# Rotary embedding on one core: the first slab loaded by one transfer instead of four

## The chip, the core and the metric

The kernel runs on one core of a Trainium2 chip. The metric is the device time of one execution in microseconds (us); three executions of the kernel before gave 164.84, 165.05 and 165.22 us, median 165.05. One of them, the 164.84 us one, was also recorded by the hardware profiler, and every line of the profile here is from it.

## The reference

`x` has 16 batches, 512 positions and 1024 values, which are 16 heads of 64; `cos` and `sin` are 512 x 32. All are float32, and so is the output.

```python
x = x.reshape(batch, seq, num_heads, head_dim)
x1, x2 = x[..., :half_dim], x[..., half_dim:]
cos = cos[None, :, None, :]
sin = sin[None, :, None, :]
rotated = np.concatenate([x1 * cos - x2 * sin,
                          x1 * sin + x2 * cos], axis=-1)
```

Every value is read once, takes part in two products and one sum, and is written once: 33.5 MB in and 33.5 MB out.

## The kernel before

**Tiling.** Two batches (`nb` = 2) make a slab: 1024 positions, of which each of the 128 partitions holds 8 in a row. A slab's row in one partition is 8 x 1024 floats, 32 KB, and lies in one piece in memory; a slab is 4 MB. There are 8 slabs and 5 buffers for them (`slots` = 5), and a slab's result is written over its input in the same buffer. A slab is worked in two passes of 4 positions, 16 passes in all.

**A pass** (L130 to L147). ScalarE casts half a slab from float32 to bf16 (L124, "xb"). VectorE multiplies it by the sin table into `t2` and by the cos table in place (L137, twice), and adds the two with the halves of `t2` exchanged (L140). ScalarE casts the result back to float32 into the slab (L144). After a slab's second pass ScalarE issues the slab's store (L146), one 4 MB transfer. The cast of the next pass is issued ahead of the current one (L131), so ScalarE's order is: cast of pass i+1, cast back of pass i.

**Tables** (L80 to L115). cos and sin are loaded by GpSimd's queue (L82), cast to bf16 (L99), spread over the partitions by four small matmuls with a 0/1 matrix (L103) and copied to SBUF as [cos cos] and [sin -sin] (L109 to L115).

**Queues.** Loads of slabs 1 to 7 are issued by SyncE (SP), one transfer of 128 rows each (L65). Loads of slabs 1 to 4 are issued at the start; the load of slab s+5 is issued after the pass that ends slab s (L148), and waits until the store of slab s has landed, since it goes into the same buffer. Stores are issued by ScalarE's queue. Each queue runs in order; transfers of the two queues share 16 DMA engines.

**The first slab** (L69 to L75). Its load is cut into four transfers by rows: the 64 even rows on SP's queue, rows 7, 15, 23, ... (16 rows) on ScalarE's queue, rows 1, 5, 9, ... (32 rows) and then rows 3, 11, 19, ... (16 rows) on SP's queue. All four go into the one tile `slab[0]`, and the first cast waits for all of them.

Of the kernel before, what the change touches and what calls it, by code (L numbers as in the profile page):

```python
# [2 lines left out]

# [4 lines left out]


@with_exitstack  # L10
def kernel(
    ctx: ExitStack,
    tc: tile.TileContext,
    x: bass.AP,
    cos: bass.AP,
    sin: bass.AP,
    num_heads: int,
    out: bass.AP,
):
    nc = tc.nc  # L20
    P = nc.NUM_PARTITIONS

    batch, seq, dim = x.shape
    nh = num_heads
    hd = dim // nh
    half = hd // 2
    bf16 = mybir.dt.bfloat16
    f32 = mybir.dt.float32

    nb = 2  # L30
    slots = 5
    nslabs = batch // nb
    rpp = nb * seq // P
    W = rpp * dim
    SP = seq // rpp
    rows = 4
    PW = rows * dim
    TW = rpp * half

    out_flat = out.rearrange("b s h d -> b s (h d)")  # L40

    singles = ctx.enter_context(tc.tile_pool(name="singles", bufs=1))
    slabs = ctx.enter_context(tc.tile_pool(name="slabs", bufs=slots))
    tpool = ctx.enter_context(tc.tile_pool(name="tpool", bufs=3))
    t2pool = ctx.enter_context(tc.tile_pool(name="t2pool", bufs=2))
    psum = ctx.enter_context(tc.tile_pool(
        name="psum", bufs=1, space=bass.MemoryType.PSUM))


    def dram(t, s, a=0, n=W):  # L50
        return bass.AP(tensor=t.tensor, offset=t.offset + s * nb * seq * dim + a,
                       ap=[[W, P], [1, n]])


    def view(t, offset, *dims):
        return dataclasses.replace(t, offset=t.offset + offset,
                                   ap=[t.ap[0], *[list(d) for d in dims]])


    slab = {}  # L60


    def load(s):
        slab[s] = slabs.tile([P, W], f32, tag="slab", name="slab")
        nc.sync.dma_start(out=slab[s], in_=dram(x, s))  # L65

    slab[0] = slabs.tile([P, W], f32, tag="slab", name="slab")  # L69
    for q, first, step in ((nc.sync, 0, 2), (nc.scalar, 7, 8),  # L70
                           (nc.sync, 1, 4), (nc.sync, 3, 8)):
        q.dma_start(  # L72
            out=slab[0][first::step, :],
            in_=bass.AP(tensor=x.tensor, offset=x.offset + first * W,
                        ap=[[step * W, P // step], [1, W]]))  # L75


    TR = seq // P
    G = rpp // TR
    raw = singles.tile([P, 2 * TR * half], f32, tag="raw")  # L80
    for i, src in enumerate((cos, sin)):
        nc.gpsimd.dma_start(out=view(raw, i * TR * half, (1, TR * half)), in_=bass.AP(  # L82
            tensor=src.tensor, offset=src.offset,
            ap=[[TR * half, P], [1, TR * half]]))

    for s in range(1, slots):
        load(s)


    pick = singles.tile([P, G * P], bf16, tag="pick")  # L90
    nc.gpsimd.memset(pick, 0.0)  # L91
    for g in range(G):
        part = view(pick, g * P, (SP, P // SP), (1, SP))
        nc.gpsimd.affine_select(  # L94
            out=part, in_=part, compare_op=mybir.AluOpType.not_equal, fill=1.0,
            base=-g, pattern=[[0, P // SP], [-G, SP]], channel_multiplier=1)

    tab1 = singles.tile([P, 2 * TR * half], bf16, tag="tab1")
    nc.vector.tensor_copy(out=tab1, in_=raw)  # L99
    acc = psum.tile([P, 2 * TW], f32, tag="acc")  # L100
    for i in range(2):
        for g in range(G):
            nc.tensor.matmul(view(acc, i * TW + g * TR * half, (1, TR * half)),  # L103
                             view(pick, g * P, (1, P)),
                             view(tab1, i * TR * half, (1, TR * half)),
                             start=True, stop=True)

    tab = singles.tile([P, 2 * rpp * hd], bf16, tag="tab")
    nc.vector.tensor_copy(out=view(tab, 0, (hd, 2 * rpp), (1, half)),  # L109
                          in_=view(acc, 0, (half, 2 * rpp), (1, half)))  # L110
    nc.vector.tensor_copy(out=view(tab, half, (hd, rpp), (1, half)),  # L111
                          in_=view(acc, 0, (half, rpp), (1, half)))
    nc.vector.tensor_scalar_mul(  # L113
        out=view(tab, rpp * hd + half, (hd, rpp), (1, half)),
        in0=view(acc, TW, (half, rpp), (1, half)), scalar1=-1.0)  # L115


    xb = {}


    def cast(u):
        s, k = u
        xb[u] = tpool.tile([P, PW], bf16, tag="xb", name="xb")
        nc.scalar.copy(out=xb[u], in_=view(slab[s], k * PW, (1, PW)))  # L124

    passes = [(s, k) for s in range(nslabs) for k in range(rpp // rows)]
    cast(passes[0])
    for i, u in enumerate(passes):  # L130
        if i + 1 < len(passes):  # L131
            cast(passes[i + 1])
        s, k = u
        xs, xu = slab[s], xb.pop(u)
        t2 = t2pool.tile([P, PW], bf16, tag="t2")
        for t, a in ((t2, rpp * hd), (xu, 0)):
            nc.vector.tensor_mul(  # L137
                out=t, in0=xu,
                in1=view(tab, a + k * rows * hd, (hd, rows), (0, nh), (1, hd)))
        nc.vector.tensor_add(  # L140
            out=xu, in0=xu,
            in1=view(t2, half, (hd, rows * nh), (-half, 2), (1, half)))

        nc.scalar.copy(out=view(xs, k * PW, (1, PW)), in_=xu)  # L144
        if k == rpp // rows - 1:
            nc.scalar.dma_start(out=dram(out_flat, s), in_=xs)  # L146
            if s + slots < nslabs:  # L147
                load(s + slots)  # L148


# [1 line left out]
_INS = ['x', 'cos', 'sin', 'num_heads']  # L152
_OUTS = [((16, 512, 16, 64), 'float32')]

_NUMBERS = {'num_heads': 16}


# [26 lines left out]
```

## Time and profile before

| | |
|---|---|
| time, median of 3 | 165.05 us |
| the profiled execution | 164.84 us |
| its span, first to last instruction | 162.9 us |
| around the span | 1.94 us |
| VectorE busy | 111.3 us, 68% |
| ScalarE busy | 114.8 us, 70% |
| TensorE, GpSimd busy | 0.6 us, 2.3 us |
| DMA | 67.24 MB, mean 413 GB/s over the span |
| one cast, either way | 3.60 us, 32 of them |
| one VectorE operation of a pass | 2.29 us, 48 of them |

The page of the profile gives busy times by engine, the span in 40 slices with the DMA engines' busy share and rate, the DMA queues (q1 is SP's, q10 ScalarE's, q0 GpSimd's), the chain of work that ended last, groups of instructions, and DMA issues. Answers on a stretch of the span are of three kinds: windows (busy time of each engine, the DMA engines' busy share and rate, where a DMA packet counts wholly in the window in which it starts), a timeline, and the chain in order of time. DMA packets of this kernel are rows: one 32 KB row is one packet on one of the 16 DMA engines.

### The profile page before, as it was taken

What the parts mean: (1) busy time and instruction counts of PE and PEld (TensorE: products, weight loads), DVE (VectorE), ACT (ScalarE), POOL (GpSimd) and SP (SyncE); (2) the same over time, 40 slices, a digit from 0 to 9 for tenths busy, and PEclk for the clock granted to TensorE, in tenths of its full rate; (3) what the DMA queues carried; (4) which work ended last, traced back from release to release, by engine and by line L of the source; (5) the groups of instructions that cost most, each with busy time, mean ns of one, the idle gap of its engine ahead of it and who ended that gap; (6) DMA issues with size and microseconds to landing.
All of it is one profiled execution on the core that took longest, in us unless ns stands there. A gap on an engine that the chain in (4) does not pass through costs nothing.

```text
span 162.9 us, 188 instructions
## 1 busy us (share of the span) xinstructions
PE 0.6 (0%) x4; PEld 0.4 (0%) x4; DVE 111.3 (68%) x52; ACT 114.8 (70%) x33; POOL 2.3 (1%) x9
## 2 busy tenths in 40 slices
PE   0000000000000000000000000000000000000000
PEld 0000000000000000000000000000000000000000
DVE  0003069999899999999999999907996099940000
ACT  0000997779999999999999999169980899553000
POOL 5000000000000000000000000000000000000000
DMA  5999899898998998998989989989989899899893
GB/s 169 354 410 258 386 491 410 386 515 386 402 499 386 451 451 386 483 418 386 515 386 402 499 386 443 459 386 491 410 386 515 386 410 491 386 459 443 386 491 153
DMA packets 2416, 67.24 MB, mean 413 GB/s; under 512 B 336, under 2 KB 336, under 8 KB 368
## 3 DMA queue, kind: packets, MB, share of 16 engines
q10 hardware_dynamic: 1184, 34.08, 49.0%
q1 hardware_dynamic: 1168, 33.03, 48.5%
q0 software_dynamic: 64, 0.13, 0.3%
HBM read 33.69 MB, written 33.55 MB: 413 GB/s over the span
## 4 chain that ended last, share of the span: by engine, by line
DMA 45%; ACT 25%; DVE 13%; issue 6%; SPq 1%; ACTq 0%
DMA slab<-in_x_dram 25%; DMA out_dram<-slab 21%; ACT slab L144 15%; ACT xb L124 9%; DVE t L137 4%; DVE xb L140 4%; DVE xb L137 4%; ACT L124 1%; SPq L72 1%; ACTq L144 0%; ACTq L124 0%; SPq L65 0%
## 5 line engine op out<-in xcount | busy, mean ns | idle before, releaser
L124 ACT CAST xb<-slab 128x4096 bf16<-128x4096 f32 x16 | 57.5, 3601 | 11.0 <-DMA slab<-in_x_dram 11.0
L144 ACT CAST slab<-xb 128x4096 f32<-128x4096 bf16 x16 | 57.7, 3603 | 5.5 <-DVE xb L140 5.3
L137 DVE TENSOR_TENSOR t<-xb,tab 128x4096 bf16<-128x4096 bf16 x16 | 36.7, 2292 | 19.6 <-ACT xb L124 19.2
L140 DVE TENSOR_TENSOR xb<-xb,t 128x4096 bf16<-128x4096 bf16 x16 | 36.7, 2292 | 0.5
L137 DVE TENSOR_TENSOR xb<-xb,tab 128x4096 bf16<-128x4096 bf16 x16 | 36.7, 2292 | 0.5
L124 ACT ACT_TABLE_LOAD x1 | 1.3, 1283 | 16.7 <-DMA slab<-in_x_dram 16.7
L99 DVE CAST tab<-raw 128x256 bf16<-128x256 f32 x1 | 0.3, 294 | 11.7 <-DMA raw<-in_sin_dram 11.7
L109 DVE CAST tab<-acc 128x512 bf16<-128x512 f32 x1 | 0.7, 691 | 0.7 <-PE acc L103 0.7
L82 POOL DMA_DIRECT2D raw<-in_cos_dram x1 | 0.7, 677 | 0.8 <-POOLq L165 0.8
L103 PE MATMUL acc<-tab,pick 128*128 128x128 bf16 x4 | 0.6, 302 | 12.0 <-DVE tab L99 12.0
L94 POOL TENSOR_SCALAR_AFFINE_SELECT pick<-pick 128x128 bf16<-128x128 bf16 x2 | 0.5, 289 | 0.1
L82 POOL DMA_DIRECT2D raw<-in_sin_dram x1 | 0.5, 534 | 0.0
L103 PEld LDWEIGHTS <-pick 128*128 128x128 bf16 x4 | 0.4, 128 | 11.9 <-issue 8.7
L111 DVE CAST tab<-acc 128x256 bf16<-128x256 f32 x1 | 0.4, 415 | 0.0
L113 DVE TENSOR_SCALAR tab<-acc 128x256 bf16<-128x256 f32 x1 | 0.4, 414 | 0.0
L91 POOL MEMSET pick<- 128x256 bf16 x1 | 0.3, 330 | 0.0
L165 POOL MEMSET const-bfloat16-1.0<- 128x1 bf16 x1 | 0.1, 103 | 0.0
L165 POOL MEMSET const-float32-0.0<- 128x1 f32 x1 | 0.1, 99 | 0.2 <-issue 0.2
L165 POOL MEMSET const-uint8-127<- 128x1 uint8 x1 | 0.1, 102 | 0.0
L165 POOL MEMSET const-float32-1.0<- 128x1 f32 x1 | 0.1, 99 | 0.0
## 6 DMA issues: line engine op xcount, KB each, us to landing
out_dram<-slab ACTq DMA_DIRECT2D x8, 4096.0 KB, 28.2
slab<-in_x_dram SPq DMA_DIRECT2D x7, 4096.0 KB, 25.7
slab<-in_x_dram SPq DMA_DIRECT2D x1, 2048.0 KB, 10.7
slab<-in_x_dram SPq DMA_DIRECT2D x1, 1024.0 KB, 12.8
slab<-in_x_dram ACTq DMA_DIRECT2D x1, 512.0 KB, 9.2
slab<-in_x_dram SPq DMA_DIRECT2D x1, 512.0 KB, 14.6
raw<-in_cos_dram POOLq DMA_DIRECT2D x1, 64.0 KB, 8.9
raw<-in_sin_dram POOLq DMA_DIRECT2D x1, 64.0 KB, 9.7
```

Of the source, the lines that this page charges most:

```text
L72: q.dma_start(out=slab[0][first::step, :], in_=bass.AP(tensor=x.tensor, offset=x.offset + first * W, ap=[[step * W, P // step], [1, W]]))
L82: nc.gpsimd.dma_start(out=view(raw, i * TR * half, (1, TR * half)), in_=bass.AP(tensor=src.tensor, offset=src.offset, ap=[[TR * half, P], ...
L94: nc.gpsimd.affine_select(out=part, in_=part, compare_op=mybir.AluOpType.not_equal, fill=1.0, base=-g, pattern=[[0, P // SP], [-G, SP]], c ...
L103: nc.tensor.matmul(view(acc, i * TW + g * TR * half, (1, TR * half)), view(pick, g * P, (1, P)), view(tab1, i * TR * half, (1, TR * half)) ...
L109: nc.vector.tensor_copy(out=view(tab, 0, (hd, 2 * rpp), (1, half)), in_=view(acc, 0, (half, 2 * rpp), (1, half)))
L111: nc.vector.tensor_copy(out=view(tab, half, (hd, rpp), (1, half)), in_=view(acc, 0, (half, rpp), (1, half)))
L113: nc.vector.tensor_scalar_mul(out=view(tab, rpp * hd + half, (hd, rpp), (1, half)), in0=view(acc, TW, (half, rpp), (1, half)), scalar1=-1.0)
L124: nc.scalar.copy(out=xb[u], in_=view(slab[s], k * PW, (1, PW)))
L137: nc.vector.tensor_mul(out=t, in0=xu, in1=view(tab, a + k * rows * hd, (hd, rows), (0, nh), (1, hd)))
L140: nc.vector.tensor_add(out=xu, in0=xu, in1=view(t2, half, (hd, rows * nh), (-half, 2), (1, half)))
L144: nc.scalar.copy(out=view(xs, k * PW, (1, PW)), in_=xu)
L165: nc = _bacc.Bacc("TRN2", target_bir_lowering=False, num_devices=1)
```

## The change

The four transfers of the first slab become one of 128 rows on SP's queue, by the same function that loads the other slabs. Nothing else differs: `t2` has two buffers before and after.

```diff
-    slab[0] = slabs.tile([P, W], f32, tag="slab", name="slab")
-    for q, first, step in ((nc.sync, 0, 2), (nc.scalar, 7, 8),
-                           (nc.sync, 1, 4), (nc.sync, 3, 8)):
-        q.dma_start(
-            out=slab[0][first::step, :],
-            in_=bass.AP(tensor=x.tensor, offset=x.offset + first * W,
-                        ap=[[step * W, P // step], [1, W]]))
+    load(0)
```

`load(s)` is the function at L63: it takes a slab buffer and issues `nc.sync.dma_start(out=slab[s], in_=dram(x, s))`.

In the compiled order of instructions VectorE, TensorE and GpSimd have the same instructions in the same order as before. SP issues five whole-slab loads at the start in place of three pieces and four loads. ScalarE's queue loses its one load, and its table load (the instruction ahead of its first cast) no longer has a wait for three of the four pieces in front of it; the wait for the slab stands at the first cast.

## The prediction

> **What bounds the kernel now.** I began with the page's slices, because neither VectorE (68%) nor ScalarE (70%) is busy enough to set the time. Lines of slices and queues:
>
> ```profile
> DMA  5999899898998998998989989989989899899893
> GB/s 169 354 410 258 386 491 410 386 515 386 402 499 386 451 451 386 483 418 386 515 386 402 499 386 443 459 386 491 410 386 515 386 410 491 386 459 443 386 491 153
> ...
> q10 hardware_dynamic: 1184, 34.08, 49.0%
> q1 hardware_dynamic: 1168, 33.03, 48.5%
> q0 software_dynamic: 64, 0.13, 0.3%
> ```
>
> The reader is to see that the 16 DMA engines are busy from about 2 us to the end: 49.0 + 48.5 + 0.3 = 97.8% of the span. So only three things can move the time: when the DMA engines start, when they run dry, and how long a row takes on them. The fourth slice (12.2 to 16.3 us), 258 GB/s, is the one slow slice inside a busy stretch. I therefore cut the span into windows whose edges fall between rounds; a **round** is one 32 KB row on each of the 16 engines, 0.524 MB. The last columns are the DMA engines' busy share and GB/s:
>
> ```profile
> 2.00:5.15 3.15, 0.00 (x0) 0.10 (x1) 0.00 (x0) 0.00 (x0) 1.30 (x4) 1.00 0.97 333
> 5.15:7.00 1.85, 0.00 (x0) 0.00 (x0) 0.00 (x0) 0.00 (x0) 0.00 (x0) 1.00 1.14 283
> 7.00:12.95 5.95, 0.59 (x4) 0.32 (x3) 0.59 (x2) 0.00 (x0) 0.00 (x0) 1.00 0.96 375
> 12.95:14.95 2.00, 0.00 (x0) 0.00 (x0) 1.05 (x3) 0.00 (x0) 0.00 (x0) 1.00 1.09 262
> 14.95:16.80 1.85, 0.00 (x0) 0.00 (x0) 0.00 (x0) 0.12 (x1) 0.00 (x0) 1.00 0.92 283
> 16.80:36.20 19.40, 0.00 (x0) 0.00 (x0) 14.52 (x7) 16.44 (x6) 0.00 (x0) 1.00 1.00 432
> ...
> 148.00:161.20 13.20, 0.00 (x0) 0.00 (x0) 0.00 (x0) 0.00 (x0) 0.00 (x0) 1.00 0.93 400
> ```
>
> From 16.80 to 36.20, whole slabs alone move 432 x 19.4 = 8.38 MB, 16 rounds, so a **normal round takes 19.4 / 16 = 1.21 us**. Ahead of 16.80 there are rounds that take far longer with the engines fully busy: the engines are held up inside rows, not waiting for work. A row's time in a window of one round is its share x its length: 1.14 x 1.85 = 2.11 us in the second line. That round is ScalarE's transfer, by the queue line of the same window:
>
> ```profile
> DMA packets 16, 0.52 MB, mean 283 GB/s; under 512 B 0, under 2 KB 0, under 8 KB 0
> ...
> q10 hardware_dynamic: 16, 0.52, 114.0%
> ```
>
> Last I read the end. The chain of waits goes through load 7, its two passes and the last cast:
>
> ```profile
> 101.00 25.66 DMA slab<-in_x_dram
> ...
> 144.36 3.60 ACT slab L144
> ```
>
> The last store is issued at 148.00. From there to 161.20 the engines still move 400 x 13.2 = 5.28 MB; the last store is 4.19 MB. So 1.09 MB of the store before it, two rounds that have yet to start and one that is running, keep the engines busy until about 151.5: the end is set by the engines' total work, and the chain through load 7 has about 3.5 us, less the delay from issue to first row, in hand. That delay, by the first load (issued at 0.74, first rows in the window that begins at 2.00), is about 1.4 us: **2.1 us in hand**.
>
> **The change, part by part.**
>
> *The two 16-row pieces go.* In rounds, the first slab takes: even rows 4, ScalarE's piece 1, rows 1::4 two, rows 3::8 one, 8 in all. By order in the queue, 12.95 to 14.95 is the round of rows 3::8 and 14.95 to 16.80 the first of slab 1, which starts unevenly behind it.
> - ScalarE's round: 2.11 - 1.21 = 0.90 us lost.
> - Rows 3::8: 1.09 x 2.00 = 2.18; lost 0.97.
> - The round behind: 0.92 x 1.85 = 1.70; lost 0.49.
> - 7.00 to 12.95: q1's four rounds there take 87.4% of 5.95 = 5.20 us in place of 4.85; 0.35 lost. The tables' small packets run in it and are not removed; I give 0.10 of it to them and 0.25 to the round behind ScalarE's.
>
> Sum: 0.90 + 0.97 + 0.49 + 0.25 = **2.6 us**. Only the 16-row pieces, on two different queues, have slow rounds; the 64 rows, the 32 rows and the whole slabs do not, so I charge the shape, not the queue or the moment. The new load has the shape of slabs 1 to 4, 16 rounds of which ran at 1.21. Nothing hides this loss and nothing hides its return, as all later rounds follow without a hole.
>
> [...]
>
> *The first round stays.* The window 2.00 to 5.15 holds two rounds in 3.15 us, where 2.42 would do: up to 0.7 us of starting cost. The whole-slab load has no row at a cold start. Below, it could start like an even-rows load and cost the same; a gain of 0.6 if that start is also of the split's making; a loss of 0.6 if 128 rows take twice as long to get going. SP's issue instruction took 0.56 to 0.59 us for 64, 32 and 16 rows alike, so I take 0.
>
> *Issues.* SP issues three fewer (about 0.6 us each), so loads 1 to 4 are queued some 2 us earlier; the queue in front of them is never empty, so this is worth nothing. ScalarE loses an issue of 0.57 us, which lies in a wait of 16 us: nothing.
>
> *The compute chain moves by more than the transfers.* ScalarE's timeline:
>
> ```profile
> 16.68 1.28 ACT L124 ACT_TABLE_LOAD   x1 [16.68 <-DMA slab<-in_x_dram]
> 17.97 7.11 ACT L124 CAST xb<-slab 128x4096 bf16<-128x4096 f32 x2
> 26.21 3.60 ACT L124 CAST xb<-slab 128x4096 bf16<-128x4096 f32 x1 [1.13 <-DMA slab<-in_x_dram]
> ...
> 38.88 0.35 ACTq L146 DMA_DIRECT2D out_dram<-slab  x1
> ```
>
> Slab 0's rows end, by rounds: two by about 5.3, six more at 1.21, 0.5 for the tables' packets: 13.1; slab 1's landing stood 0.7 behind its last row, so 13.8 in place of 16.6. The 1.28 us table load leaves the path, as it no longer stands behind a wait. First cast: 13.8 instead of 17.97, 4.2 earlier; VectorE's tables, ready at 14.0 before, are wanted at 17.4. The first store is issued at about 34.7, 4.2 earlier, and thus 1.6 us (one to two rounds) earlier in the stream of transfers. From there the queues take turns, so loads 3 to 7 end one or two rounds later in the stream: load 7 lands 2.6 - 1.2 = 1.4, or 2.6 - 2.4 = 0.2 us, earlier than before. The last store's issue follows it by 21.3 us as now: 146.6 or 147.8. Its first row is due at 151.5 - 2.6 = 148.9 and can start 1.4 behind the issue, at 148.0 or 149.2. So this is hidden, or costs 0.3.
>
> Forecast: 164.84 - 2.6 = 162.2 for the profiled execution; that one stands 0.2 below the median of its three, so **162.4** for the median.
>
> **Rivals.**
> 1. *Part of it stays.* ScalarE's slow round may be the first use of its queue, and come back with the first store: 0.90 + 0.25 kept, 165.05 - 1.46 = 163.6. For: it is the queue's first transfer. Against: the other 16-row piece is as slow on a queue long in use.
> 2. *The tail shows.* Load 7 comes two or three rounds later in the stream: the last store starts 0.3 to 1.5 late, 162.7 to 163.9. For: 2.1 us in hand is little.
> 3. *The change does not do it.* The slow rounds belong to the moment (tables' packets, PSUM copies from 12.65 to 14.0) and stay: 165.0, no change. Against: VectorE is busier later with rounds at 1.21.
> 4. *Slower.* The same tail, further: the first store comes so early that load 7 is pushed back by five rounds or more in the stream: 126.65 - 2.6 + 5 x 1.21 = 130.1, the last store's issue 151.4, first row 152.8 in place of 151.5: 166.4. It decides from about 4.2 rounds. For: each round that the first store gains pushes load 7 back by one. Against: that takes a first store some 6 us earlier in the stream, and VectorE's chain lets it gain 1.6.
>
> **How the numbers follow.** Forecast 0.70, rival 1 0.10, rival 2 0.09, rival 3 0.06, rival 4 0.05. Changes under 0.2% (0.33 us) are about what a measurement of this kernel cannot tell from none. Faster 0.89, same 0.06, slower 0.05. The range takes in the forecast with the starting round's 0.6 either way, most of rival 2 and rival 1: 161.6 to 163.6.
>
> **What would show it.** After: one 4 MB issue for slab 0, landed at about 13.8; the table load before 2 us; no slice under 350 GB/s between 4 and 150 us, windows from 5.3 to 17 us near 430 GB/s; the first store issued near 34.7, the last near 147, with the engines busy without a hole to about 158.5; span near 160.3. I am wrong if a round of 2 us appears at the start or at the first store, if the first rows start after 2.1 us, or if the DMA engines idle ahead of the last store.

## The result and the profile after

| | before | after |
|---|---|---|
| median | 165.11 us (6 runs, 164.84 to 165.22) | 162.53 us (6 runs, 162.28 to 162.89) |
| ratio | | 0.9848, 95% interval 0.9834 to 0.9862 |
| profiled execution, span | 164.84, 162.9 | 162.89, 160.8 |
| ScalarE, VectorE busy | 114.8, 111.3 | 114.8, 111.3 |

The gain is 2.58 us by the medians and 1.95 us by the two profiled executions: the one of before is the fastest of its six, the one of after the slowest of its six. No engine does less work, so the gain has to be in the stream of transfers. The slices of the page after, first:

```profile
DMA  6999999999999999999999999999999999999993
GB/s 220 448 408 399 473 432 399 473 432 318 416 432 456 408 432 456 416 432 456 416 432 456 416 424 440 440 416 432 456 408 432 465 408 432 456 416 432 456 416 171
```

The slow fourth slice (258 GB/s before) is gone. In its place one dent is new: the tenth slice, 36.2 to 40.2 us, with 318 GB/s. Windows of the changed kernel, cut between rounds, show both (last columns: the DMA engines' busy share, GB/s):

```profile
1.70:4.70 3.00, 0.00 (x0) 0.10 (x1) 0.00 (x0) 0.32 (x1) 1.60 (x5) 1.00 1.05 350
4.70:12.30 7.60, 0.59 (x4) 0.32 (x3) 0.47 (x2) 0.00 (x0) 0.00 (x0) 1.00 1.00 431
12.30:31.70 19.40, 0.00 (x0) 0.00 (x0) 15.67 (x10) 15.15 (x5) 0.00 (x0) 1.00 1.00 432
31.70:35.40 3.70, 0.00 (x0) 0.00 (x0) 3.63 (x3) 3.70 (x2) 0.00 (x0) 1.00 0.99 425
35.40:36.80 1.40, 0.00 (x0) 0.00 (x0) 1.40 (x1) 1.40 (x1) 0.00 (x0) 1.00 0.96 374
36.80:38.50 1.70, 0.00 (x0) 0.00 (x0) 1.32 (x2) 1.70 (x2) 0.00 (x0) 1.00 1.23 308
```

From 4.70 to 12.30 us, 431 x 7.6 = 3.28 MB pass: six rounds (3.15 MB) and the tables' 0.13 MB, in the time of normal rounds, where the kernel before had its slow ones. The last two lines are the dent: the row that starts on each engine between 36.80 and 38.50 takes 1.23 x 1.70 = 2.09 us. It stands where the first store arrives, just ahead of its rows: the queue lines of 35.40 to 38.50 us show loads alone (q1, two rounds), and the first row of the store starts at 38.75.

```profile
q1 hardware_dynamic: 32, 1.05, 110.4%
```

ScalarE's timeline of the changed kernel:

```profile
0.74 1.28 ACT L117 ACT_TABLE_LOAD   x1 [0.74 <-PEq L158]
13.50 7.11 ACT L117 CAST xb<-slab 128x4096 bf16<-128x4096 f32 x2 [11.48 <-DMA slab<-in_x_dram]
...
34.41 0.38 ACTq L139 DMA_DIRECT2D out_dram<-slab  x1
```

A tally by rounds splits the profiled difference. I count 32 KB rows by their starts in the trace, 16 to a round, and take the mean start of each round. "Nine rounds" is from the first round to the tenth; "18 rounds" is from the 28th round, ahead of any store, to the 46th; in the later part of both traces, loads and stores mixed, 18 rounds take 21.78 or 21.79 us wherever one begins. The last column is the mean end of the last 16 rows.

| | first round | nine rounds | 18 rounds (normal: 21.79) | end of the last 16 rows |
|---|---|---|---|---|
| before | 2.34 | 14.68 | 21.80 | 161.13 |
| after | 1.97 | 11.94 | 22.78 | 158.98 |

So 2.74 us are saved in the first nine rounds, 0.37 by a first round that starts earlier, and 0.99 are lost again around the first store: 2.74 + 0.37 - 0.99 = 2.12, against 161.13 - 158.98 = 2.15.

That is a mean over the 16 engines, and the time ends with the last of them. The last row of all ended at 161.31 us before and at 159.59 after, only 1.72 apart, since it came 0.18 us behind the mean before and 0.61 after. Behind it, SP closes the kernel with a row of instructions that wait, one after the other, for the kernel's transfers and engines. Lines of the two profiles for these waits (the last two of the eight are the final meeting of all engines):

```profile
L179 SPq EVENT_SEMAPHORE  x8: 17/28/28, 161.7 to 162.8; - x8
...
L172 SPq EVENT_SEMAPHORE  x8: 17/28/28, 125.4 to 160.8; - x8
```

Before, the last store is waited for in the first of the other six, so all six come behind it, 0.06 us apart. After, it is waited for in the sixth, and the five ahead of it have passed long ago. From the last row to the end of the span are 1.59 us before and 1.23 after, and 1.72 + 0.36 = 2.08 is the difference of the spans. So 0.36 us of the gain are not in the rounds of the transfers at all.

The end of the chain behaves as before. In order of time:

```profile
98.21 27.15 DMA slab<-in_x_dram
...
143.06 3.60 ACT slab L137
```

Load 7 lands at 125.36 instead of 126.65, and the last store is issued at 146.70 instead of 148.00. Its first rows start at 149.30 in the mean, behind the rows of the store before and without a hole, so the tail stays covered.

### The profile page after: what moved, and what is told of

The parts are those of the page before. It is cut to its first block, busy times and chain, and to the rows that moved or that the text cites. A ratio compares the mean times of both kernels' runs of the same rounds, so it can differ in the third digit from the quotient of the medians.

```text
span 160.8 us, 182 instructions
## 1 busy us (share of the span) xinstructions
PE 0.6 (0%) x4; PEld 0.4 (0%) x4; DVE 111.3 (69%) x52; ACT 114.8 (71%) x33; POOL 2.3 (1%) x9
## 4 chain that ended last, share of the span: by engine, by line
DMA 47%; ACT 25%; DVE 13%; issue 6%; ACTq 0%; SPq 0%
DMA slab<-in_x_dram 25%; DMA out_dram<-slab 22%; ACT slab L137 16%; ACT xb L117 9%; DVE xb L133 4%; DVE t L130 4%; DVE xb L130 4%; ACTq L137 0%; SPq L65 0%
## 5 line engine op out<-in xcount | busy, mean ns | idle before, releaser
L96 PEld LDWEIGHTS <-pick 128*128 128x128 bf16 x4 | 0.4, 128 | 11.4 <-issue 8.2
```

## Experiments

Two questions: is it the 16-row pieces that cost, and what is the loss at the first store? My first theory for the second was the prediction's rival 1, a first use of ScalarE's queue.

**1. All four pieces on SP's queue** (the kernel before).

```diff
-    for q, first, step in ((nc.sync, 0, 2), (nc.scalar, 7, 8),
+    for q, first, step in ((nc.sync, 0, 2), (nc.sync, 7, 8),
```

> The kernel before with its 16 rows 7, 15, 23, ... issued on SP's queue instead of ScalarE's; the four pieces and their shapes stay. My theory (the shape of 16 rows with a step of 8 makes the slow rounds; beside it ScalarE's queue has a cost of its first use, about 1.0 us, which the changed kernel pays at its first store): both 16-row rounds stay at 2.1 to 2.2 us, the first store now shows a loss of 0.5 to 1.0 us, time 165.1 + 0.5 to 1.0 = 165.6 to 166.1. Rival (ScalarE's slow round was nothing but the first use of its queue): the round of rows 7::8 falls to 1.21, the first store takes the loss over, time 164.9 to 165.2.

Measured: 165.06 us, ratio to before 1.0 (0.9991 to 1.0009). Windows of its trace; the first line is the round of rows 7::8, now on SP's queue, the next the round behind it:

```profile
7.97:9.91 1.94, 0.00 (x0) 0.00 (x0) 0.00 (x0) 0.00 (x0) 0.00 (x0) 1.00 1.19 291
9.91:11.76 1.85, 0.00 (x0) 0.00 (x0) 0.00 (x0) 0.00 (x0) 0.00 (x0) 1.00 0.90 283
```

The share of the first, 1.19 x 1.94 = 2.31, holds a few of the tables' packets; the round's rows take 2.19 us in the mean, and those of the next 0.90 x 1.85 = 1.67. The pair is as slow on the other queue. The shape half of my theory holds. The other half falls: ScalarE's queue is first used by the first store here, and the 18 rounds around it take 21.80, no loss.

**2. Three pieces, none of 16 rows, one on ScalarE's queue.**

```diff
-    for q, first, step in ((nc.sync, 0, 2), (nc.scalar, 7, 8),
-                           (nc.sync, 1, 4), (nc.sync, 3, 8)):
+    for q, first, step in ((nc.sync, 0, 2), (nc.scalar, 1, 4),
+                           (nc.sync, 3, 4)):
```

> The kernel before with three pieces instead of four: rows 0::2 (64) on SP, rows 1::4 (32) on ScalarE's queue, rows 3::4 (32) on SP. No piece has 16 rows; the load is still split over two queues. My theory (shape, not splitting): no round of 2 us, rounds of 1.21 from about 4 us on, and no loss at the first store since ScalarE's queue has been used: 161.5 to 162.6, as fast as the changed kernel or up to 1.0 us faster. Rival (splitting over two queues costs by itself): a slow round where ScalarE's piece runs, 163.5 to 165. Second rival (a first use of ScalarE's queue costs about 1 us wherever it comes): about 162.5, with the loss at the start instead of at the first store.

Measured: 163.46 us, ratio 0.990 (0.9883 to 0.9917). Most of the gain is there with the load still cut and still on two queues (1.52 us, where the changed kernel gains 2.22 on the same chip, experiment 4): nine rounds take 11.91, and ScalarE's two rounds 1.21 each. But it missed my range: the first store loses 0.67 (18 rounds in 22.46) although the queue had been used.

**3. ScalarE's queue used early in the changed kernel.**

```diff
-        nc.gpsimd.dma_start(out=view(raw, i * TR * half, (1, TR * half)), in_=bass.AP(
+        (nc.scalar, nc.gpsimd)[i].dma_start(out=view(raw, i * TR * half, (1, TR * half)), in_=bass.AP(
```

> The changed kernel with the 64 KB cos load issued on ScalarE's queue instead of GpSimd's, so that this queue has carried something before the first store. My theory (a first use of the queue costs rounds when both queues are loaded): the two long rounds ahead of the first store (1.3 and 2.1 us in the changed kernel) go to 1.21, time 162.5 - 0.5 to 1.0 = 161.5 to 162.0. Rival (the loss belongs to the first store itself, a first write to memory): the long rounds stay, 162.3 to 162.7.

Measured: 162.64 us, ratio 0.9852 (0.9835 to 0.9868); 18 rounds in 22.46, a loss of 0.67. With experiments 1 and 2 the theory of a first use is dead in both directions.

**4. The changed kernel again.**

> The changed kernel itself, profiled and timed again beside the others. My theory: 162.5 (162.2 to 162.9), slow rounds at the start gone, and a loss of 0.5 to 1.0 us at the first store again. Rival (the long rounds at the first store were an accident of the one profiled execution, the slowest of its six): rounds of 1.21 there, profiled time near 162.3.

Measured: 162.76 us (162.63 to 163.37), ratio 0.9866 (0.9848 to 0.9885); loss at the first store 0.85 (18 rounds in 22.64). The loss is no accident of one execution.

**5. Which partitions a round touches.** My theory was now that the set of rows in a round, and so the partitions they go to, decides its length. Slab 2's load in the changed kernel is cut into eight 16-row pieces.

```diff
+    load(1)
+    slab[2] = slabs.tile([P, W], f32, tag="slab", name="slab")
+    for first, step in ((32, 4), (33, 4), (34, 4), (35, 4),
+                        (96, 2), (97, 2), (0, 1), (16, 1)):
+        nc.sync.dma_start(
+            out=slab[2][first:first + 15 * step + 1:step, :],
...
+    for s in range(3, slots):
```

> The changed kernel with the load of slab 2 cut into eight pieces of 16 rows, one row on each DMA engine, in this order: four of rows 32+r, 36+r, ... 92+r (r = 0 to 3), two of every second row of 96 to 127, then rows 0 to 15 and rows 16 to 31. [...] Rival A (any 16-row transfer is slow, one row an engine): all eight rounds about 2.1. Rival B (the distance of the rows in memory decides: 256 KB in the slow pieces of the kernel before; here 128, 64 and 32 KB): the first four the slowest or all at 1.21, the last two at 1.21.

Windows of its trace, the four rounds of rows 32+r, 36+r, ... in the first line and one round in each of the others:

```profile
22.10:27.00 4.90, 0.00 (x0) 0.00 (x0) 4.90 (x3) 3.87 (x2) 0.00 (x0) 1.00 1.00 428
27.00:29.05 2.05, 0.00 (x0) 0.00 (x0) 2.02 (x2) 2.05 (x1) 0.00 (x0) 1.00 1.15 256
29.05:31.60 2.55, 0.00 (x0) 0.00 (x0) 2.55 (x2) 2.09 (x2) 0.00 (x0) 1.00 1.00 206
31.60:35.05 3.45, 0.00 (x0) 0.00 (x0) 3.42 (x2) 3.45 (x2) 0.00 (x0) 1.00 1.16 152
35.05:39.50 4.45, 0.00 (x0) 0.00 (x0) 4.03 (x3) 4.45 (x2) 0.00 (x0) 1.00 1.01 118
```

The first four rounds take 4.90 / 4 = 1.23 us each, though they too are 16 rows, one on an engine. The next two have rows of 1.15 x 2.05 = 2.36 and 2.55 us, the last two of 1.16 x 3.45 = 4.00 and 1.01 x 4.45 = 4.49. Rival A (any 16-row piece) falls with the first line. Rival B falls too: the last two rounds read rows that lie side by side in memory and are the slowest. What is left is the set of rows: three kinds of set, three lengths. Row r in memory always goes to partition r in this kernel, so no run separates the partitions from something that depends on the same row numbers in memory. The kernel's time, 175.09 us (one execution), is 12.6 us above the changed kernel's 162.53; the four slow rounds make 2.36 + 2.55 + 4.00 + 4.49 - 4 x 1.21 = 8.6 of it, and its loads of slabs 3 and 4 were issued only at 51.9 us, behind waits that the many pieces brought.

**6. The load of slab 4 issued later** (the changed kernel).

```diff
+        if s == slots - 1:
+            nc.gpsimd.tensor_copy(out=view(slab[s], 0, (1, 1)),
+                                  in_=view(raw, TR * half, (1, 1)))
         nc.sync.dma_start(out=slab[s], in_=dram(x, s))
```

> The changed kernel, but the load of slab 4 is issued at about 11.5 us instead of 2.8: GpSimd writes one element of that slab's buffer from the sin load, and SP waits for it. Nothing needs slab 4 before 66 us. Theory now (the loss of 0.7 to 1.0 us at the first store comes where all five slab loads are queued in the first 4 us; before and with all pieces on SP's queue the fifth was issued at 9.4 to 10.0 us and there was none): loss at the first store 0 to 0.1, time 162.6 - 0.8 = 161.6 to 162.0. Rival (the loss comes with the moment of the first store, 34.4 us, or with the undisturbed start): the long rounds stay, 162.3 to 162.9.

Measured: 162.57 us, ratio 0.9842 (0.9814 to 0.9869), load 4 issued at 11.30, loss at the first store 0.80. The theory missed.

**7. The load of slab 4 issued early** (the kernel before).

```diff
-    for q, first, step in ((nc.sync, 0, 2), (nc.scalar, 7, 8),
+    for q, first, step in ((nc.sync, 0, 2), (nc.gpsimd, 7, 8),
```

> The kernel before with the 16 rows 7, 15, 23, ... issued on GpSimd's queue, so that no load of SP has to wait and the load of slab 4 is issued at about 3.8 us instead of 9.96. Theory (early fifth load makes the loss at the first store): the slow 16-row rounds stay and a loss of 0.7 to 1.0 us at the first store appears, 165.0 + 0.8 = 165.5 to 166.1. Rival (the loss has to do with the undisturbed start or the earlier first store): no loss there, 164.8 to 165.3.

Measured: 165.17 us, ratio 0.9999 (0.9982 to 1.0016), load 4 issued at 4.33, 18 rounds in 21.80: no loss. With experiment 6 the number of early loads is out.

**8. Three pieces, and load 4 later**: the edits of 2 and 6 together.

> The split into 64, 32 (ScalarE's queue) and 32 rows with the load of slab 4 issued at about 11.5 us in the same way. Theory (16-row pieces and the early fifth load are all that matters, splitting by itself costs nothing): no slow round and no loss at the first store, 161.6 to 162.4. Rival (the split over two queues costs something else, since that kernel measured 163.46): 162.7 to 163.3.

Measured: 163.26 us, ratio 0.9876 (0.9851 to 0.9901); loss at the first store 0.87. The rival's range holds.

**9. Two tiny loads ahead of slab 1** (the changed kernel).

```diff
     load(0)
+    spare = singles.tile([P, 32], f32, tag="spare")
+    for i in range(2):
+        nc.sync.dma_start(out=view(spare, i * 16, (1, 16))[:16], in_=bass.AP(
+            tensor=x.tensor, offset=x.offset, ap=[[16, 16], [1, 16]]))
```

> The changed kernel with two loads of 1 KB (16 pieces of 64 bytes into a spare tile, used by nothing) on SP's queue between the loads of slab 0 and slab 1, which puts four more descriptors in front on each DMA engine. What was left: in all kernels with a loss at the first store the long rounds were rows 4 to 6 of slab 3 on SP's queue, 31 to 33 descriptors from its start, and in the three without a loss that place in the queue was passed one to five rounds earlier against the first store. Theory (the loss is where the first store meets that place in SP's queue): the loss goes, 162.6 - 0.7 = 161.7 to 162.1. Rival (the loss is the first store's, in a stream that had no 16-row piece): it stays, 162.4 to 162.9.

Measured: 163.12 us, ratio 0.9864 (0.9838 to 0.9889); loss 0.97. The time is over both ranges, on a chip whose kernel before took 165.39. The loss stays, so a place in SP's queue is not it.

**10. The first store later** (the changed kernel).

```diff
+    late = t2pool.tile([P, PW], bf16, tag="t2")
+    nc.scalar.copy(out=late, in_=view(slab[0], 0, (1, PW)))
     cast(passes[0])
```

> The changed kernel with one more cast of 3.6 us on ScalarE ahead of the first (its result is used by nothing), so that compute and the first store come 3.6 us later, at about 38.0 us, five rounds into slab 3. Theory (a place in SP's queue, 35.8 to 39 us): the long rounds stay there or vanish, and none at 39 to 43. Rival (the arrival of the first store's descriptors, about 1 us behind its issue): long rounds move to 39 to 43. In both the time stays at 162.0 to 163.0, since the last store, which has about 1 us in hand, is not held by the first pass: load 7 then lands some three rounds earlier in the stream.

Measured: 163.28 us, ratio 0.9876 (0.9849 to 0.9904). The time is over my 163.0 (same chip as experiment 9). The first store was issued at 40.74, later than I had said, since ScalarE's casts came in another order. Windows of its trace:

```profile
30.60:41.50 10.90, 0.00 (x0) 0.00 (x0) 10.90 (x6) 10.07 (x3) 0.00 (x0) 1.00 1.01 433
41.50:45.50 4.00, 0.00 (x0) 0.00 (x0) 3.96 (x3) 2.39 (x1) 0.00 (x0) 1.00 1.04 393
```

Up to 41.5 us, past the place of the dent in the changed kernel, all is at full rate; the slow stretch now lies behind the store's issue again: 393 x 4.0 = 1.57 MB, three rounds, in 4.0 us instead of 3.6. The loss belongs to the arrival of the first store. The last store was issued at 147.97 and its first rows start at 149.43 in the mean; the rounds there run on without a hole. So 1.46 us from issue to first rows are enough, and the changed kernel, with 149.30 - 146.70 = 2.60, had 1.1 us or more in hand.

**11. Three pieces, all on SP's queue**: the edit of 2 with `nc.sync` for the second piece.

> The split into 64, 32 and 32 rows, all three pieces on SP's queue. No piece of 16 rows, no second queue. My theory (only 16-row pieces cost): no round of 2 us in the first slab, 162.4 to 163.0, as the changed kernel. Rival (cutting the slab into pieces costs by itself, as the two kernels with the 32-row split, 163.46 and 163.26, would have it): 163.1 to 163.6.

Measured: 163.14 us, ratio 0.9873 (0.9848 to 0.9897), beside 163.12 of experiment 9 on the same chip. Nine rounds in 11.90, none of 2 us; loss at the first store 0.74. The time lies at the lower end of the rival's range and above mine, so my theory missed; but the kernel of experiment 9, whose first slab is not cut, is level with it.

**12. The four pieces in slab 1 instead of slab 0** (all on SP's queue). Two things had gone together so far: a 16-row piece of step 8 ahead of the first store, and no loss there (0.01 us each in the kernel before, 1 and 7; 0.59 to 0.99 in the nine profiles without such a piece).

```diff
-    for s in range(1, slots):
+    slab[1] = slabs.tile([P, W], f32, tag="slab", name="slab")
+    for first, step in ((0, 2), (1, 4), (3, 8), (7, 8)):
+        nc.sync.dma_start(
+            out=slab[1][first::step, :],
...
+    for s in range(2, slots):
         load(s)
```

> The changed kernel with the load of slab 1 (not slab 0) cut into 64, 32, 16 (3, 11, 19, ...) and 16 (7, 15, 23, ...) rows, all on SP's queue. [...] Theory (the two go together: a stream that had such a piece before the first store does not pay at the first store): slow rounds in slab 1, two of about 2.2 and the one behind, cost 1.5 to 2.7; no loss at the first store, 162.8 + 1.5 to 2.7 - 0.8 = 163.5 to 164.7. [...]

Measured: 164.46 us, ratio 0.9961 (0.9947 to 0.9975). With a loss at the first store as well, the expected sum would be 162.8 + 1.5 to 2.7 = 164.3 to 165.5, so the time lies in both ranges; the rounds decide, and they are as the theory said. Windows of its trace: the two 16-row rounds, the round behind them, and the stretch in which the first store (issued at 34.38) arrives:

```profile
19.65:21.56 1.91, 0.00 (x0) 0.00 (x0) 1.91 (x1) 0.93 (x1) 0.00 (x0) 1.00 1.15 275
21.56:23.90 2.34, 0.00 (x0) 0.00 (x0) 2.34 (x3) 0.00 (x0) 0.00 (x0) 1.00 1.01 224
23.90:25.89 1.99, 0.00 (x0) 0.00 (x0) 1.99 (x2) 0.00 (x0) 0.00 (x0) 1.00 0.86 263
25.89:37.90 12.01, 0.00 (x0) 0.00 (x0) 4.73 (x3) 10.18 (x3) 0.00 (x0) 1.00 1.01 437
```

Rows take 2.20, 2.36 and 1.71 us in the first three windows: (2.20 - 1.21) + (2.36 - 1.21) + (1.71 - 1.21) = 2.64 us, about the 2.74 that the two pieces cost in slab 0. And the first store costs nothing: 18 rounds in 21.79.

The loss at the first store, over all kernels but 5, whose pieces were still running then (18 rounds, less 21.79):

| kernel | first store issued | loss |
|---|---|---|
| before; 1; 7; 12 (with 16-row pieces of step 8) | 38.88; 39.30; 39.86; 34.38 | 0.01; 0.01; 0.01; 0.00 |
| after; 4; 2; 3; 6; 8; 9; 11 (without) | all from 34.39 to 36.07 | 0.99; 0.85; 0.67; 0.67; 0.80; 0.87; 0.97; 0.74 |
| 10 (without) | 40.74 | 0.59 |

## Why the prediction was right

**What bounds the kernel**: right. Compute work is the same, and the time moved with the rounds, but for the 0.36 us behind the last row.

**The two 16-row pieces**: right in cause. The estimate was 2.6 us; the first nine rounds are 2.74 shorter. Experiment 1 (another queue), experiment 12 (another slab) and experiment 5 (other rows in pieces of the same size) show that it is the set of rows in a round: neither the queue, nor the moment, nor the number of rows. Why some sets are slow is not shown: it can be the partitions or the same row numbers in memory (experiment 5). Experiments 2, 8 and 11 keep a cut load without such pieces and keep most of the gain. Rival 3 is out. The second queue brought nothing here: with all four pieces on SP's queue the time is 165.06 us, ratio 1.0 (experiment 1).

**The first round stays**: nearly. It is 0.37 us earlier in the profiled pair, which I had put at zero between -0.6 and 0.6. The first round started at 2.25 to 2.38 in the kernels whose first transfer has 64 rows and at 1.89 to 2.16 in those that begin with the whole slab, so cutting does cost here; the kernels 1 and 11 have it on one queue, so a second queue is not needed for it.

**Issues**: SP issues two fewer at the start and not three (three pieces and four loads became five loads), so loads 1 to 3 were issued 1.4 to 1.6 us earlier and not 2. The term is zero either way.

**The compute chain**: right in each step. Table load at 0.74, first cast at 13.50 (13.8 predicted), first store at 34.41 (34.7), load 7 landed 1.3 us earlier (1.4 or 0.2), last store at 146.70 (146.6 or 147.8). No hole at the tail; rivals 2 and 4 did not occur, and experiment 10 measures what was in hand.

**What the sum lacked**: a term for the first store. I named it as a sign of being wrong ("a round of 2 us appears at the start or at the first store"), and one of 2.09 us did appear, with a slice of 318 GB/s where I had said none under 350. I had it only as rival 1, and its mechanism, the first use of ScalarE's queue, is refuted by experiments 1, 2 and 3. It lacked the end too: 0.36 won in SP's last waits, 0.43 lost since the last engine ends further behind the mean. In the profiled pair the losses eat more than the 0.37 and 0.36: 1.95 measured for 2.6. The medians differ by 2.58, so that 162.53 stands beside the predicted 162.4. That closeness is partly luck: terms of both signs that I did not have, and a profiled execution at the slow end of its six. How evenly the engines end varies from run to run as well: in experiment 4's profile the last 16 rows end 0.11 us earlier in the mean than in the first profile of the same kernel, the last row 0.46 later, and the time is 0.48 longer.

**What stays open.** The loss at the first store occurred in all nine profiles without a 16-row piece of step 8 before it and in none of the four with one; experiment 12 was made for that and agreed. Why such a piece pays for it in advance is not shown. The starts of a round spread over 0.67 us before the first store and 1.04 after it in the changed kernel, and stay at 0.36 in the kernel before, as if the engines were pushed apart once. But in experiment 1 they spread over 0.68 us, as widely as in the changed kernel, and nothing was lost, and in experiments 3 and 6 the spread grew by only 0.04 us or less, with a loss of 0.67 and 0.80.

Kernels 2 and 8 came out 0.7 us above the whole-slab kernels of the same chips (4 and 6), while 11 and 9 were level. By one profile of each, 0.2 to 0.4 of it is the later first round, and 0.3 lies behind the last row: five of SP's waits and 1.51 to 1.52 us there in 2 and 8, one wait and 1.23 to 1.24 in 4 and 6. Kernel 9, with its two extra loads, has five waits and 1.50 us, like 11 (1.53). No version tried beats the changed kernel by more than its runs vary.

## What to carry to other kernels

When the DMA engines are busy from end to end, look for rows that take longer, not for idle time: cut the span between rounds, and compare bytes and time of each piece with a clean stretch. In these runs a load cut by rows kept the rate of its rounds with some sets of rows and lost it with others, and neither their number nor their step told which. 64 rows of step 2, 32 rows of step 4 and 16 rows of step 4 (32, 36, ... 92) ran at full rate, 1.21 to 1.27 us a round but for the very first one (1.80 before, 1.91 after) and those right behind a slow one (1.49 and 1.69 before); 16 rows of step 8 (2.11 to 2.36 us), and 16 of step 2 out of one quarter (96, 98, ... 126; 2.36 and 2.55), took 1.7 to 2.1 times as long, and 16 neighbouring rows (4.00 and 4.49) 3.3 to 3.7 times. Differences of 0.3 us came from the two ends as well: from the first transfer's start, and from where the last store stands among SP's last waits. An instruction that left the head of the compute chain (the 1.28 us table load) was worth nothing here, where the transfers had the last word: experiment 10 puts 3.6 us there, and its last rows end at 159.16 us, beside 158.94 and 159.06 in 9 and 11 on the same chip.

## What the runs showed of the hardware

- A 32 KB row took 1.21 us on a DMA engine, 432 GB/s over 16 engines for loads alone (12.30 to 31.70 us of the changed kernel), and the same when loads and stores took turns (434 GB/s from 41.77 to 125.00 us, 17.83 MB on SP's queue and 18.32 on ScalarE's).
- SP's queue worked in order: before, its transfers for slabs 0 to 4, issued at 0.74, 1.35, 1.98, 2.61, 3.25, 3.75 and 9.96 us, landed at 11.4, 14.1, 16.6, 26.2, 35.9, 49.3 and 68.6.
- Rounds of 16 rows took 1.23, 2.36 to 2.55 and 4.00 to 4.49 us, in eight pieces of equal size on one queue that differ in their rows and their place in the order (experiment 5).
- The first store into a running stream of loads cost 0.6 to 1.0 us in nine profiles, and nothing in the four of kernels that had sent 16-row pieces of step 8 before.
- From the end of the last row to the end of the span were 1.23 to 1.24 us with one of SP's waits behind that row (changed kernel; 4, 6, 10), 1.29 with two (5), 1.38 with three (3), 1.50 to 1.53 with five (2, 8, 9, 11) and 1.53 to 1.60 with six or seven (before; 1, 7, 12).
